# Queue order of the loads from the up projection into the first chunk of the down projection, and another order of one half unit's products

## Chip, cores and metric

One Trainium2 chip, one of its cores. The time is device microseconds of one execution of the whole layer; the kernel before takes 1906.95 us (median of 3 runs, 1906.23 to 1907.41).

## What is computed

One encoder layer on 512 tokens of width 2048, all in float32: attention and pooling with their projections, and a feed-forward part. The change lies in the feed-forward part:

```python
h = rms_norm(x, pre_ffn_g[l])
up = causal_dwconv(h @ w_up[l], conv_w[l], conv_b[l])
y = (jax.nn.gelu(up[..., :D_FF], approximate=True) * up[..., D_FF:]) @ w_down[l]
x = x + rms_norm(y, post_ffn_g[l])
```

Here `w_up` is 2048 x 11264 (`D_FF` is 5632) and `w_down` is 5632 x 2048.

## The kernel before

**Split products.** Every float32 product is made of three passes of TensorE: each factor is split into a rounded high part (ScalarE, L143) and the low rest (VectorE, L144), and `mm3` adds high x high (L159), low x high (L160) and high x low (L161). In the up projection from half unit 4 on, L947 and L953 do the same with wider matmuls for products 3 to 7.

**Up projection.** The output columns are cut into 88 half units (number k, from 0), each 128 channels, two half units to a unit. Each half unit is a 2 x 2 block product done with seven products instead of eight (Strassen's scheme in Winograd's form), numbered i = 1 to 7; below, (k, i) is product i of half unit k. The factor on the side of the weights is a block of `w_up`, or a sum of blocks. A buffer `wx` gets the block (1,1) by a plain DMA of the SP queue (L786), then further blocks by accumulating DMAs of the POOL queue (L795), each of which can start only when the split that reads the sum so far is done. So `wx` serves (k,4) or (k,5), then (k,6), then (k,3). Likewise `wy` holds (k,1), `wz` (k,2), `wv` the factor of (k,7) for k below 5, `ww` a plain copy for (k,4) in the first half units, and `wu` a plain copy that VectorE adds to `wx` or `wv` (L803) for (k,3) of half units 1, 2 and 3; in half units 2 and 3 it also adds `ww` to `wv` (L801). For half units 0 and 4 the last block of `wx` came by an accumulating DMA instead; from half unit 5 on VectorE adds `wz`.

**Order of the work.** `Factors.order` lists the products by hand; TensorE follows it, and each product's factor is split four products ahead (`AHEAD`), its loads asked for some six further ahead (`LOOK`). Half unit 4 is number `EARLY - 1`, the fifth: there the products go over from halves of single PSUM banks to pairs of banks, which VectorE must first have emptied (L1182 is the last reading of one of them). TensorE's order is written in the program; those of VectorE, ScalarE and the queues come from a scheduler that places the instructions by its own estimate, unless `tc.issue_after(x)` holds an instruction behind another. Each engine and each queue works in its order: an instruction that waits holds up all behind it. A load waits for its buffer: `raw4` has 6 of them, `wx` from half unit 2 on has 3.

**Down projection.** `w_down` is worked off in chunks, of which the first is chunk 0, with the same seven products in two column halves cc. `right` loads a factor of the weights (`b`, 1 MB each, from `in_w_down` or from sums made ahead in DRAM, `wd_sum`; L645 and L652), `left` and `first_left` load the gate products (`gc` and `a`, from `gd`; L1296 and L1197). The buffers of `b` come from a ring of 3 (`raw1`) and one of 2 (`raw2`). `ORDER0` gives the order for chunk 0: (0,1), (0,2), (1,1), (1,2), then 5, 7, 6, 3, 4 of each half. The first two products begin while the last products of half unit 87 are being finished on VectorE.

Of the kernel before, what the change touches and what calls it, by code (L numbers as in the profile page):

```python
# [30 lines left out]
EARLY = 5  # L31
# [46 lines left out]
def encoder_layer(ctx: ExitStack, tc: tile.TileContext, x, xT, vecs, rel, post_mix, post_ffn,  # L78
# [7 lines left out]
    nc = tc.nc  # L86
# [114 lines left out]
    def qk_specs(h):  # L201
        return halves(f"q{h}", w_in, head_cols("q", h), 8, P), halves(f"k{h}", w_in, head_cols("k", h), 8, P)
# [8 lines left out]
    for h in range(1, HEADS):  # L211
        q, k = qk_specs(h)
# [51 lines left out]
    for kb in range(KD):  # L264
        i, o = divmod(kb, 8)
# [329 lines left out]
    gd = [[dram.tile([P, CU, 2, H], F32, name=f"gd{c}_{i}") for i in range(2)] for c in range(NC)]  # L595
# [12 lines left out]
    def right_tile(tag, name, dt=F32R):  # L608

        n = turns[tag] = turns.get(tag, -1) + 1  # L610
        if later and n % (2 + LATER[tag]) >= 2:
            return later[tag](name, dt)
        return pr.tile([P, CU, S], dt, tag=tag, bufs=2, name=name)
# [3 lines left out]
    def raw1(name, dt=F32):  # L617
        return right_tile("raw1", name, dt)

    def w_block(j, l, c=0, cs=slice(0, C)):  # L620
        r = 256 * CU * c
        return w_down[r:r + 256 * CU, l * C + cs.start:l * C + cs.stop].rearrange(
            "(u j p) n -> p u j n", j=2, p=P)[:, :, j, :]

    wd_sum = {i: dram.tile([P, CU, C], F32, name=f"wd_sum{i}") for i in (5, 7, 6, 4)}
# [14 lines left out]
    def right(c, cc):  # L640
        cs = slice(cc * S, (cc + 1) * S)

        def load(j, l, ring=None):
            b = (ring or (later["raw2"] if j else raw1))(f"b{j}{l}")
            nc.sync.dma_start(b, w_block(j, l, c, cs))  # L645
            return b

        def first_chunk(i):
            if i in (1, 2):
                return ahead.pop((cc, i), None) or load(i - 1, 0, later[f"raw{i}"] if cc else raw1)  # L650
            b = (raw1 if i in (7, 3) else later["raw2"])(f"b{i}")
            nc.sync.dma_start(b, w_block(1, 1, c, cs) if i == 3 else wd_sum[i][:, :, cs])  # L652
            return b

        b = {}
        order = yield
        while True:
            i = order
            if i < 0:
                ahead[cc, -i] = first_chunk(-i)  # L660
                order = yield
                continue
            if c == 0:
                v = first_chunk(i)
            else:
                for jl in {1: (11, 12), 5: (11, 12), 7: (22,), 6: (22,), 3: (22,), 2: (21,), 4: (21,)}[i]:
                    if jl not in b:
                        b[jl] = load(jl // 10 - 1, jl % 10 - 1)
                for n, into, other in ((5, 11, 12), (7, 12, 22), (6, 11, 22), (4, 21, 11)):
                    if i == n:  # L670
                        nc.vector.tensor_add(b[into], b[into], b[other])  # L671
                v = b[{1: 11, 5: 11, 7: 12, 6: 11, 2: 21, 3: 22, 4: 21}[i]]
            hi, lo = right_tile("wh", "bh"), right_tile("wl", "bl")
            split(hi, lo, v)
            order = yield hi, lo
# [50 lines left out]
    class Factors:  # L726
# [3 lines left out]
        def __init__(self):  # L730
            n = 2 * NU

            self.order = [(k, i) for k in range(EARLY) for i in (1, 2)]
            self.order += [(0, 5), (0, 7), (1, 5), (0, 6), (1, 7), (1, 6), (0, 3), (1, 3), (0, 4), (1, 4)]
            self.order += [(j, i) for i in (4, 7, 5, 6, 3) for j in (2, 3)]
            for k in range(EARLY - 1, n):
                late = [(k - 1, 6), (k - 1, 3)]
                if k < EARLY:
                    o = [(k, 4), (k, 7), (k, 5)]
                elif k == n - 1:  # L740
                    o = [(k, 4), (k, 1), (k, 5), (k, 2), *late, (k, 6), (k, 7)]
                else:
                    o = [(k, 4), (k, 1), (k, 2), *late, (k, 5), (k, 7)]
                self.order += o
            self.order += [(n - 1, 3)]
            self.last = n - 1
            self.alone = *range(EARLY), n - 1
            self.raw, self.made, self.loaded, self.used = {}, [], 0, 0
            self.held = {"x": [], "r": []}
            self.homes = []  # L750
# [21 lines left out]
            self.add(k, "x", 1, 0)  # L772

        def load(self, k, i):
            what = "u" if i == 3 and k in (1, 2, 3) else self.source(k, i)
            if (k, what) in self.raw:
                return True
            in_x = what == "x" and k >= 2 or what == "w" and k == self.last
            held, n = (self.held["x"], 3) if in_x else (self.held["r"], 6)
            if len(held) >= n and held[-n] in self.raw:  # L780
                return False
            if in_x and p3 is None:
                return False
            held.append((k, what))
            v = raw_x("wx") if in_x else raw4("w" + what)
            self.last_load = nc.sync.dma_start(v, self.block(k, *self.LOADS[what])).ins  # L786
            self.raw[k, what] = v
            if what == "x" and k in self.alone:
                self.add(k, "x", 1, 0)
            if what == "v":  # L790
                self.add(k, "v", 0, 0)
            return True
# [4 lines left out]
        def make(self, k, i):  # L797
            early, what = k < EARLY, self.source(k, i)
            v = self.raw[k, what]
            if i == 6 and k in (2, 3):  # L800
                nc.vector.tensor_add(v, v, self.raw.pop((k, "w")))  # L801
            if i == 3 and k not in (0, 4):
                nc.vector.tensor_add(v, v, self.raw.pop((k, "u" if early else "z")))  # L803
            hi, lo = self.homes.pop(0) if self.homes else (w4("wfh"), w4("wfl"))
            split(hi, lo, v)
            if i == 4 and k not in self.alone:
                self.add(k, "x", 1, 0)
            elif i == 1 and not early:
                self.add(k, "y", 1, 0)
            elif i == 5 and k not in (2, 3):  # L810
                self.add(k, "x", 0, 0)
            elif i == 6 and k in (0, 4):
                self.add(k, "x", 0, 1)
            elif not (i == 6 or i == 2 and not early or i in (4, 7) and k in (2, 3)):
                del self.raw[k, what]
            self.made.append(tuple(v.rearrange("p (a b) -> p a b", a=8) for v in (hi, lo)))
# [32 lines left out]
    def raw_x(name):  # L849
        return p3.tile([P, 1024], F32, tag="x", bufs=3, name=name)  # L850
# [115 lines left out]
    with tc.tile_pool(name="p2", bufs=1, reuse_waits="tile") as p2:  # L966
# [112 lines left out]
        for n in (5, 3):  # L1079
            B = new_banks(f"m{n}", 4 if n == 5 else 0)  # L1080
            for cc in range(2):
                late = (lambda q: h0.append(next(turning))) if n == 3 else None
# [110 lines left out]
    def first_left():  # L1193

        def load(i, j):
            v = raw4(f"a{i}{j}").rearrange("p (u n) -> p u n", u=CU)
            nc.sync.dma_start(v, gd[0][i][:, :, j, :])  # L1197
            return v

        def parts(v):  # L1200
            hi, lo = (w4(f"a{p}").rearrange("p (u n) -> p u n", u=CU) for p in "hl")
            split(hi, lo, v)
            return hi, lo

        for j in range(2):
            yield parts(load(0, j))
# [68 lines left out]
    with tc.tile_pool(name="p4", bufs=2, reuse_waits="tile") as p4:  # L1275
# [16 lines left out]
        def left(c):  # L1292

            def load(i):
                g = half_g(f"gc{i}")
                nc.sync.dma_start(g, gd[c][i])  # L1296
                return [g[:, :, j, :] for j in range(2)]

            i = yield
            a11, a12 = load(0)  # L1300
            v, state = {1: a11, 2: a12, 3: a12}, None
            while True:
                if 7 not in v and (c or i not in (1, 2)):
                    a21, a22 = load(1)
                    s = scratch("s")
                    v.update({5: s, 7: a21, 6: s, 4: a22})
                if i in (5, 7) and state is None:
                    nc.vector.tensor_sub(s, a22, a21)
                    state = "n1"
                if i == 5 and state == "s2" or i == 6:  # L1310

                    nc.vector.scalar_tensor_tensor(s, s, -1.0, a11, op0=ALU.mult, op1=ALU.subtract)
                    state = "n1" if i == 5 else "s2"
                if i == 7:
                    nc.vector.tensor_sub(a21, a11, a21)
                if i == 3:
                    nc.vector.scalar_tensor_tensor(a12, a12, -1.0, s, op0=ALU.mult, op1=ALU.subtract)
                hi, lo = slot_h("ah", F32R), slot_l("al", F32R)
                split(hi, lo, v[i])
                i = yield hi, lo  # L1320
# [201 lines left out]
```

## Time and profile before

| what | value |
|---|---|
| median of 3 runs | 1906.95 us |
| profiled execution, its own time | 1911.16 us |
| its span, first to last instruction | 1909.2 us |
| mean granted TensorE clock | 0.993 |
| busy: VectorE | 1467.1 us, 77% |
| busy: ScalarE | 952.6 us, 50% |
| busy: POOL | 302.4 us, 16% |
| moved by DMA | 403.55 MB, mean 211 GB/s |

Times in the rows of the profile are microseconds from the span's start. A row of a timeline gives start, length, engine, line, operation, output and inputs, shapes, how many, and in brackets the idle time of the engine before it with what ended that. SPq and POOLq are the two DMA queues; "landing" is the time from issuing a DMA to its completion.

### The profile page before, as it was taken

Reading aid. Unit: us, or ns where it says so; the run is one execution under the profiler, and the core shown is the slowest. Engines: PE = TensorE matmul, PEld = TensorE weight load, DVE = VectorE, ACT = ScalarE, POOL = GpSimd, SP = SyncE. Lnnn points to the kernel's source line nnn. Section 1 sums busy time; section 2 is a strip of 40 time slices with the busy share of each in tenths; the row PEclk is TensorE's granted clock in tenths of the full one; section 3 lists DMA queues with packets and bytes.
Section 4 is the critical chain, followed back from the end, with each engine's and each line's share of the span. In section 5 each row is a group of like instructions: output and inputs, shape, how many; then the busy total and the mean of one; then the engine's idle time right before and its main releaser. Section 6 shows DMA issues by size and latency. Waiting matters only on the chain.

```text
span 1909.2 us, 26467 instructions
## 1 busy us (share of the span) xinstructions
PE 1873.5 (98%) x10298; PEld 1633.0 (86%) x10298; DVE 1467.1 (77%) x1742; ACT 952.6 (50%) x1174; POOL 302.4 (16%) x397
## 2 busy tenths in 40 slices
PE   9999999999999899999999999999998899999998
PEld 7888888888889889999999999999997688888886
DVE  5554346587688778888888888888888789998877
ACT  6333233355487445455455554455444555465543
POOL 4000000000001111111221112121110112222221
PEclk9999999999999989999999999999999999999999
DMA  9747948577877878788898889789776989999998
GB/s 329 216 116 177 246 110 207 142 192 222 279 278 193 233 162 202 201 195 189 196 202 223 195 184 222 191 185 203 178 167 208 326 242 250 251 221 240 222 225 236
DMA packets 181949, 403.55 MB, mean 211 GB/s; under 512 B 11584, under 2 KB 63168, under 8 KB 179264
## 3 DMA queue, kind: packets, MB, share of 16 engines
q0 software_dynamic: 47488, 144.72, 41.2%
q1 hardware_dynamic: 134336, 257.14, 40.9%
q8 instruction: 81, 1.33, 0.3%
q14 instruction: 44, 0.36, 0.1%
HBM read 345.19 MB, written 106.95 MB: 237 GB/s over the span
## 4 chain that ended last, share of the span: by engine, by line
PE 87%; DVE 5%; DMA 3%; issue 2%; ACT 2%; POOL 0%; SPq 0%; POOLq 0%; DVEq 0%; ACTq 0%
PE q L947 18%; PE q L953 9%; PE p L161 6%; PE p L159 6%; PE p L160 6%; PE q L160 6%; PE q L159 6%; PE q L161 6%; PE m L160 2%; PE m L159 2%; PE m L161 2%; PE u L160 2%; PE v L160 2%; PE u L161 2%; PE v L159 2%
## 5 line engine op out<-in xcount | busy, mean ns | idle before, releaser
L143 ACT ACTIVATE wfh<-wx 128x1024 fp32r<-128x1024 f32 x167 | 172.9, 1058 | 216.4 <-DVE wx L803 133.7
L947 PE MATMUL q<-h,wfh 128*128 128x512 f32 x960 | 255.7, 395 | 4.0 <-DVE z L1182 4.0
L144 DVE TENSOR_TENSOR wfl<-wx,wfh 128x1024 fp32r<-128x1024 f32 x167 | 200.7, 1221 | 57.9 <-ACT wfh L143 57.9
L159 PE MATMUL p<-bh,ah 128*128 128x512 f32 x560 | 219.2, 392 | 9.0 <-ACT ah L143 7.6
L161 PE MATMUL p<-bh,al 128*128 128x512 f32 x560 | 219.2, 391 | 3.3 <-DVE al L144 3.3
L160 PE MATMUL p<-bl,ah 128*128 128x512 f32 x560 | 218.8, 391 | 0.0
L159 PE MATMUL q<-gT,wfh 128*128 128x256 f32 x752 | 213.2, 283 | 1.1 <-DVE z L910 1.1
L161 PE MATMUL q<-gT,wfl 128*128 128x256 f32 x752 | 213.1, 283 | 0.9 <-DVE wfl L144 0.9
L160 PE MATMUL q<-gT,wfh 128*128 128x256 f32 x752 | 213.1, 283 | 0.0
L947 PEld LDWEIGHTS q<-h,wfh 128*128 128x128 f32 x960 | 176.6, 190 | 34.0 <-issue 4.3
L143 ACT ACTIVATE bh<-b 128x2048 fp32r<-128x2048 f32 x70 | 133.7, 1917 | 82.8 <-DVE b L671 51.3
L947 PE MATMUL q<-gT,wfh 128*128 128x512 f32 x640 | 169.4, 396 | 4.3 <-ACT wfh L143 3.2
L144 DVE TENSOR_TENSOR bl<-b,bh 128x2048 fp32r<-128x2048 f32 x70 | 159.5, 2287 | 13.8 <-PE p L160 7.4
L795 POOL DMA_DIRECT2D wx<-in_w_up x88 | 77.3, 878 | 547.2 <-DVE wfl L144 449.6
L160 PEld LDWEIGHTS q<-gT,wfh 128*128 128x128 f32 x752 | 142.3, 189 | 1.9 <-DVE gT L144 0.2
L159 PEld LDWEIGHTS q<-gT,wfh 128*128 128x128 f32 x752 | 142.4, 189 | 1.3 <-ACT wfh L143 1.3
L161 PEld LDWEIGHTS q<-gT,wfl 128*128 128x128 f32 x752 | 142.3, 189 | 1.3 <-DVE wfl L144 1.3
L947 PEld LDWEIGHTS q<-gT,wfh 128*128 128x128 f32 x640 | 119.7, 192 | 25.7 <-ACT wfh L143 3.5
L953 PEld LDWEIGHTS q<-h,wfl 128*128 128x128 f32 x960 | 131.8, 192 | 9.5
L143 ACT ACTIVATE wfh<-wy 128x1024 fp32r<-128x1024 f32 x82 | 87.1, 1062 | 102.6 <-PE q L953 66.0
L953 PE MATMUL q<-h,wfl 128*128 128x256 f32 x960 | 134.7, 283 | 0.0
L159 PEld LDWEIGHTS p<-bh,ah 128*128 128x128 f32 x560 | 105.6, 189 | 32.1 <-ACT ah L143 8.9
(441 smaller groups left out, 4132.2 us busy)
## 6 DMA issues: line engine op xcount, KB each, us to landing
wx<-in_w_up POOLq DMA_DIRECT2D x88, 512.0 KB, 7.4
b<-in_w_down SPq DMA_DIRECT2D x38, 1024.0 KB, 8.5
sum<-part POOLq DMA_DIRECT2D x70, 512.0 KB, 8.1
wx<-in_w_up SPq DMA_DIRECT2D x45, 512.0 KB, 4.2
wy<-in_w_up SPq DMA_DIRECT2D x44, 512.0 KB, 7.6
wz<-in_w_up SPq DMA_DIRECT2D x44, 512.0 KB, 3.8
wy<-in_w_up POOLq DMA_DIRECT2D x39, 512.0 KB, 7.7
wo_sum<-in_w_o POOLq DMA_DIRECT2D x16, 1024.0 KB, 12.0
```

The source lines that it names most:

```text
L143: rounded = nc.scalar.activation(hi, src, AF.Copy)
L144: nc.vector.tensor_sub(lo, src, f32(hi))
L159: nc.tensor.matmul(ps, l[0], r[0], start=first, stop=False)
L160: nc.tensor.matmul(ps, l[0], r[1], start=False, stop=False)
L161: nc.tensor.matmul(ps, l[1], r[0], start=False, stop=last)
L795: self.last_add = nc.gpsimd.dma_start(self.raw[k, what], self.block(k, m, kh), accum_op=ALU.add).ins
L947: nc.tensor.matmul(ps.rearrange("p (a b) -> p a b", a=2), w[0][:, kb], both(h_f[i], kb), start=kb == 0, stop=kb == 7)
L953: nc.tensor.matmul(ps[:, :T], w[1][:, kb], at(h_f[i], kb)[0], start=False, stop=False)
```

## The change

`in_turn` issues a DMA of the SP queue behind the one that it issued last, so that these DMAs stand in the queue in the order in which the program asks for them. All loads of `Factors.load`, of `first_left`, and those of `right` and `left` for chunk 0 go through it. In `Factors.order`, (4,5) and (5,4) move ahead of (4,7). For (4,3), `wu` is loaded by the SP queue, and VectorE adds it to `wx`; the accumulating DMA after (4,6) is gone. Nothing else changes; lines of the program from L625 on move down by 8.

```diff
+    def in_turn(dest, src):
+
+        with tc.issue_after(in_turn.last):
+            in_turn.last = nc.sync.dma_start(dest, src).ins
+        return in_turn.last
+
+    in_turn.last = load_w.last
+
...
         def load(j, l, ring=None):
             b = (ring or (later["raw2"] if j else raw1))(f"b{j}{l}")
-            nc.sync.dma_start(b, w_block(j, l, c, cs))
+            (nc.sync.dma_start if c else in_turn)(b, w_block(j, l, c, cs))
             return b
...
             b = (raw1 if i in (7, 3) else later["raw2"])(f"b{i}")
-            nc.sync.dma_start(b, w_block(1, 1, c, cs) if i == 3 else wd_sum[i][:, :, cs])
+            in_turn(b, w_block(1, 1, c, cs) if i == 3 else wd_sum[i][:, :, cs])
             return b
...
                 if k < EARLY:
-                    o = [(k, 4), (k, 7), (k, 5)]
+                    o = [(k, 4), (k, 5), (k + 1, 4), (k, 7)]
...
                 else:
-                    o = [(k, 4), (k, 1), (k, 2), *late, (k, 5), (k, 7)]
+                    o = [(k, 4), (k, 1), (k, 2), *late, (k, 5), (k, 7)][k == EARLY:]
...
-            what = "u" if i == 3 and k in (1, 2, 3) else self.source(k, i)
+            what = "u" if i == 3 and k in (1, 2, 3, 4) else self.source(k, i)
...
-            self.last_load = nc.sync.dma_start(v, self.block(k, *self.LOADS[what])).ins
+            self.last_load = in_turn(v, self.block(k, *self.LOADS[what]))
...
-            if i == 3 and k not in (0, 4):
+            if i == 3 and k:
                 nc.vector.tensor_add(v, v, self.raw.pop((k, "u" if early else "z")))
...
-            elif i == 6 and k in (0, 4):
+            elif i == 6 and not k:
                 self.add(k, "x", 0, 1)
...
-            nc.sync.dma_start(v, gd[0][i][:, :, j, :])
+            in_turn(v, gd[0][i][:, :, j, :])
...
-                nc.sync.dma_start(g, gd[c][i])
+                (nc.sync.dma_start if c else in_turn)(g, gd[c][i])
```

How the instructions move, at three places. First the SP queue of the kernel before, from the `wv` of (2,7) and (3,7) on: `wx` of half units 2 and 3 stands between the two `wu`, then `wx` of 4, 5 and 6 in one go, then `ww` and `wv` of half unit 4.

```order
L786 DMA wv<-in_w_up 128x1024 x2
L786 DMA wu<-in_w_up 128x1024
L786 DMA wx<-in_w_up 128x1024 x2
L786 DMA wu<-in_w_up 128x1024
L786 DMA wx<-in_w_up 128x1024 x3
L786 DMA ww<-in_w_up 128x1024
L786 DMA wv<-in_w_up 128x1024
L786 DMA wy<-in_w_up 128x1024
L786 DMA wz<-in_w_up 128x1024
```

The same stretch of the SP queue with the change: `wx` of 2 and 3, both `wu`, `ww` of 4, `wx` of 4 and 5, `wv` of 4, `wy` and `wz` of 5, then the new `wu` of 4.

```order
L623 DMA wv<-in_w_up 128x1024 x2
L623 DMA wx<-in_w_up 128x1024 x2
L623 DMA wu<-in_w_up 128x1024 x2
L623 DMA ww<-in_w_up 128x1024
L623 DMA wx<-in_w_up 128x1024 x2
L623 DMA wv<-in_w_up 128x1024
L623 DMA wy<-in_w_up 128x1024
L623 DMA wz<-in_w_up 128x1024
L623 DMA wu<-in_w_up 128x1024
L623 DMA wx<-in_w_up 128x1024
```

So `wx` of 2 and 3 moved ahead of a `wu`, and `wx` of 4 behind `ww` of 4; `wx` of 6 no longer stands ahead of `ww` and `wv`.

Second, VectorE where TensorE passes to pairs of banks, before: rows from the addition of (2,6)'s result on; `wfl<-wv` is the low part of (4,7), the two `wfl<-wx` are those of (4,5) and (5,4).

```order
L925 TENSOR_TENSOR z<-q_2_5585,z 128x512
L144 TENSOR_TENSOR wfl<-wv,wfh 128x1024
L928 TENSOR_TENSOR z<-q_2_5585,z 128x256
L925 TENSOR_TENSOR z<-q_3_5623,z 128x512
L1182 TENSOR_TENSOR z<-q_2_5524,z 128x512
L928 TENSOR_TENSOR z<-q_3_5623,z 128x256
L144 TENSOR_TENSOR wfl<-wx,wfh 128x1024
L1148 SCALAR_TENSOR_TENSOR ca<-z,vec,ca 128x511 x2
L1149 SCALAR_TENSOR_TENSOR ca<-z,vec,ca 128x510 x2
L144 TENSOR_TENSOR wfl<-wx,wfh 128x1024
```

The same rows of VectorE with the change.

```order
L933 TENSOR_TENSOR z<-q_2_5590,z 128x512
L144 TENSOR_TENSOR wfl<-wx,wfh 128x1024
L936 TENSOR_TENSOR z<-q_2_5590,z 128x256
L933 TENSOR_TENSOR z<-q_3_5623,z 128x512
L1190 TENSOR_TENSOR z<-q_2_5524,z 128x512
L936 TENSOR_TENSOR z<-q_3_5623,z 128x256
L144 TENSOR_TENSOR wfl<-wx,wfh 128x1024
L1156 SCALAR_TENSOR_TENSOR ca<-z,vec,ca 128x511 x2
L1157 SCALAR_TENSOR_TENSOR ca<-z,vec,ca 128x510 x2
L144 TENSOR_TENSOR wfl<-wv,wfh 128x1024
```

The splits of (4,5) and (5,4) took the places of those of (4,7) and (4,5), and (4,7) the third. Nine rows further on VectorE has one new row, the addition of `wu` to `wx` (L811 there, L803 before).

Third, the SP queue where the down projection begins, before, with the buffers' numbers: `b00` and `b10` of the top two rows of `b` are (0,1) and (0,2), `b3_13708` is (0,3), `b7_13825` is (1,7), `b00_13584` is (1,1), `b10_13603` is (1,2), `b5` is (0,5).

```order
L1197 DMA a00_13412<-gd0_0_3583 128x4x256
L1197 DMA a01_13472<-gd0_0_3583 128x4x256
L786 DMA wx_13072<-in_w_up 128x1024
L645 DMA b00_13280<-in_w_down 128x4x512
L645 DMA b10_13282<-in_w_down 128x4x512
L652 DMA b3_13708<-in_w_down 128x4x512
L652 DMA b7_13825<-wd_sum7_3611 128x4x512
L645 DMA b00_13584<-in_w_down 128x4x512
L1296 DMA gc0_13590<-gd0_0_3583 128x2048
L645 DMA b10_13603<-in_w_down 128x4x512
L652 DMA b5_13613<-wd_sum5_3610 128x4x512
L1296 DMA gc1_13619<-gd0_1_3584 128x2048
```

The same stretch of the SP queue with the change.

```order
L623 DMA wx_13074<-in_w_up 128x1024
L623 DMA wz_13077<-in_w_up 128x1024
L623 DMA b00_13282<-in_w_down 128x4x512
L623 DMA b10_13284<-in_w_down 128x4x512
L623 DMA a00_13414<-gd0_0_3583 128x4x256
L623 DMA a01_13474<-gd0_0_3583 128x4x256
L623 DMA b00_13586<-in_w_down 128x4x512
L623 DMA gc0_13592<-gd0_0_3583 128x2048
L623 DMA b10_13605<-in_w_down 128x4x512
L623 DMA b5_13615<-wd_sum5_3610 128x4x512
L623 DMA gc1_13621<-gd0_1_3584 128x2048
L623 DMA b7_13629<-wd_sum7_3611 128x4x512
```

The loads for (0,3) and (1,7) no longer stand ahead of those for (1,1), `gc0`, (1,2), (0,5) and `gc1`, and the two `a` moved from ahead of (0,1) and (0,2) to behind them. Between the two places, each `wx` of a half unit k now stands ahead of its own `wy` and `wz`, where before it stood ahead of those of k + 1.

## Prediction

> **What bounds it now.** I read the page first, then the windows, then TensorE's timeline where its windows are not full, and last the engines and queues that it waits for there.
>
> ```profile
> PE 1873.5 (98%) x10298; PEld 1633.0 (86%) x10298; DVE 1467.1 (77%) x1742; ACT 952.6 (50%) x1174; POOL 302.4 (16%) x397
> ```
>
> TensorE is the bound; only its idle time and its slow clock can be won. The windows (span, then busy time of PE, PEld, DVE, ACT, POOL with counts, granted clock, DMA share, GB/s) say where these lie:
>
> ```profile
> 655.00:705.00 50.00, 42.46 (x241) 37.85 (x240) 32.01 (x44) 20.99 (x25) 7.60 (x9) 0.86 0.73 166
> 1460.00:1515.00 55.00, 44.02 (x174) 33.38 (x175) 40.79 (x35) 30.07 (x29) 5.41 (x8) 0.94 0.92 322
> 850.00:950.00 100.00, 100.00 (x651) 91.50 (x651) 84.36 (x107) 50.97 (x59) 21.14 (x25) 1.00 0.87 196
> 1445.00:1460.00 15.00, 13.67 (x80) 11.81 (x79) 13.62 (x19) 9.53 (x10) 0.00 (x0) 1.00 0.10 24
> ```
>
> In 655 to 705 TensorE is idle for 7.5 us and its clock is 0.86; in 1460 to 1515 it is idle for 11.0 us. Between the two (850 to 950 stands for it) it is full. In 1445 to 1460 the DMA engines do almost nothing (share 0.10), right ahead of the second hole. TensorE's timeline in the first hole:
>
> ```profile
> 659.92 1.78 PE L947 MATMUL q<-h,wfh 128*128 128x512 f32 x7
> ...
> 666.86 3.33 PE L947 MATMUL q<-h,wfh 128*128 128x512 f32 x7 [3.98 <-DVE z L1182]
> ...
> 678.61 0.39 PE L161 MATMUL q<-gT,wfl 128*128 128x256 f32 x1 [0.39 <-DVE wfl L144]
> ...
> 684.22 1.78 PE L947 MATMUL q<-h,wfh 128*128 128x512 f32 x7
> ...
> 690.34 3.36 PE L947 MATMUL q<-gT,wfh 128*128 128x512 f32 x7 [3.16 <-ACT wfh L143]
> ...
> 701.30 2.00 PE L947 MATMUL q<-h,wfh 128*128 128x512 f32 x8
> ```
>
> (4,4) begins at 659.92. Then TensorE waits 3.98 us, and (4,7) runs at half clock (3.33 us for seven matmuls that took 1.78 before). (5,1) gets its low part at 678.61. (4,6) begins at 684.22; behind it 3.16 us are lost, and (4,3) is slow again. The last row is the end of (5,7) and the start of (6,4). Who was late, on VectorE, ScalarE, the SP queue and the POOL queue:
>
> ```profile
> 639.96 1.29 DVE L1165 TENSOR_TENSOR ca<-ca,cb 128x512 f32<-128x512 f32 x2 [2.46 <-ACT ca L1158]
> ...
> 643.77 2.35 DVE L801 TENSOR_TENSOR wv<-wv,ww 128x1024 f32<-128x1024 f32 x2
> ...
> 663.95 1.23 DVE L144 TENSOR_TENSOR wfl<-wv,wfh 128x1024 fp32r<-128x1024 f32 x1 [8.24 <-ACT wfh L143]
> ...
> 677.34 1.22 DVE L144 TENSOR_TENSOR wfl<-wy,wfh 128x1024 fp32r<-128x1024 f32 x1
> ...
> 679.61 1.22 DVE L144 TENSOR_TENSOR wfl<-wx,wfh 128x1024 fp32r<-128x1024 f32 x1
> ```
>
> ```profile
> 636.50 1.06 ACT L143 ACTIVATE wfh<-wx 128x1024 fp32r<-128x1024 f32 x1 [2.81 <-DMA wx<-in_w_up]
> ...
> 662.87 1.06 ACT L143 ACTIVATE wfh<-wv 128x1024 fp32r<-128x1024 f32 x1 [9.93 <-DMA wv<-in_w_up]
> ...
> 689.23 2.00 ACT L143 ACTIVATE wfh<-wx 128x1024 fp32r<-128x1024 f32 x2 [11.80 <-DMA wx<-in_w_up]
> ```
>
> ```profile
> 604.32 12.82 SPq L786 DMA_DIRECT2D wv<-in_w_up  x2
> 621.59 0.90 SPq L786 DMA_DIRECT2D wx<-in_w_up  x2
> ...
> 645.02 0.33 SPq L786 DMA_DIRECT2D ww<-in_w_up  x1
> ```
>
> ```profile
> 653.07 0.92 POOL L795 DMA_DIRECT2D wv<-in_w_up  x1 [9.71 <-DMA wv<-in_w_up]
> ```
>
> L1182, which (4,7) waits for, stands on VectorE behind the low part of (4,7) itself (663.95, after 8.24 us of nothing), that behind ScalarE's high part (662.87), and that waited for the accumulate on `wv` issued at 653.07: 9.8 us. (4,3) waited 11.80 us on ScalarE for the last accumulate on `wx`.
>
> **The change, part by part.** Landings (min, median, max) of the loads of `w_up` in 640 to 665 and of its accumulates in 640 to 700:
>
> ```profile
> DMA to landing us min/median/max: 4.5/5.9/8.6
> DMA to landing us min/median/max: 5.6/6.6/9.7
> ```
>
> *First gap.* L1182 now stands behind the split of (4,5), whose `wx` needs a load and one accumulate. The load comes right behind `ww`, and `ww` waits for the first of the two L801 (643.77; `ww` went out at 645.02). That L801 gets earlier: VectorE waited 2.46 us at 639.96 for ScalarE's gelu (L1158), which stood behind a high part that waited 2.81 us for `wx` of half unit 2 (636.50). That `wx` was issued at 621.59, behind a `wu`; now it follows the second `wv`, issued at 604.32 + 12.82 - 0.33 = 616.8, so it comes over 4 us earlier and the wait goes. `ww` then goes out at 642.5, `wx` of 4 at 642.9 (0.4 for one issue), lands 5.9 later; 0.4 more for the POOL queue, then the accumulate, 8.5 (near the one of 9.8, which ran beside the same loads): 657.7. VectorE starts the low part 1.1 later (as 662.87 to 663.95), at 658.8 instead of 663.95. From there to the end of the low part of (5,1) it takes what it took, 677.34 + 1.22 - 663.95 = 14.6: 673.4. TensorE could be there at 659.92 + 4 products of 2.79 (below) = 671.1, so it waits 2.3 us at (5,1), and the term is 673.4 - 678.6 = **-5.2**. Bounds: -7.5 where TensorE doesn't wait; with the gelu still late and both DMAs at their longest (645.4 + 8.6 + 0.4 + 9.7 + 1.1 = 665.2), +1.2. (5,4), now second, has a plain load, which lands before. (4,7), now third, is asked for 5.6 us later than it was, and its accumulate has that time more.
>
> *Second gap.* No accumulate is left after (4,6): VectorE adds `wu`, which has landed long before, in 1.2 us, then high part 1.0, low part 1.2. Behind the low part of (4,6) (679.61 + 1.22) that is 684.3 on the times before, and (4,3) is needed at the end of (4,6), 687.0. The addition costs nothing: ScalarE, and VectorE behind it, did nothing while waiting for 689.23. From 684.22, four products of 2.79 would end at 695.4; (6,4) began at 701.5 (its row starts with the last matmul of (5,7)). Term: **-6.1**, of which 3.16 is idle and 3.0 slow clock. Bound: if the wait of 2.3 us at (5,1) halves the clock again, -3.1. Of the idle times 3.16 halved it and 1.05 (1491.32, below) did not; 2.3 lies between, and I take none.
>
> The half units up to 87 follow with nothing moved on VectorE, ScalarE or POOL, so TensorE hands on what it has won. In the second hole, TensorE, the SP queue and VectorE:
>
> ```profile
> 1444.38 1.77 PE L947 MATMUL q<-h,wfh 128*128 128x512 f32 x7
> ...
> 1447.17 1.77 PE L947 MATMUL q<-gT,wfh 128*128 128x512 f32 x7
> ...
> 1470.62 0.39 PE L161 MATMUL p<-bh,al 128*128 128x512 f32 x1
> 1476.10 0.79 PE L159 MATMUL p<-bh,ah 128*128 128x512 f32 x1 [5.09 <-ACT ah L143]
> ...
> 1477.95 0.79 PE L161 MATMUL p<-bh,al 128*128 128x512 f32 x1 [0.34 <-DVE al L144]
> ...
> 1481.11 0.52 PE L159 MATMUL p<-bh,ah 128*128 128x512 f32 x1
> ...
> 1491.32 0.50 PE L159 MATMUL p<-bh,ah 128*128 128x512 f32 x1 [1.05 <-ACT ah L143]
> ...
> 1514.05 0.50 PE L161 MATMUL p<-bh,al 128*128 128x512 f32 x1 [0.53 <-DVE al L144]
> ```
>
> ```profile
> 1433.93 1.09 SPq L645 DMA_DIRECT2D b<-in_w_down  x2
> 1457.93 0.37 SPq L652 DMA_DIRECT2D b<-in_w_down  x1
> 1463.32 0.54 SPq L652 DMA_DIRECT2D b<-wd_sum  x1
> 1463.95 0.56 SPq L645 DMA_DIRECT2D b<-in_w_down  x1
> ```
>
> ```profile
> 1469.62 1.28 DVE L1165 TENSOR_TENSOR ca<-ca,cb 128x512 f32<-128x512 f32 x2
> 1474.47 2.29 DVE L144 TENSOR_TENSOR bl<-b,bh 128x2048 fp32r<-128x2048 f32 x1 [3.57 <-ACT bh L143]
> ```
>
> One product takes 1447.17 - 1444.38 = 2.79. The third product of the down projection, (1,1), should follow 1470.62; it waits 5.09 us for `gc0`, and the clock is low until 1481.11. The SP queue shows why: the loads for (0,3) and (1,7) waited there until 1457.93 and 1463.32 for the buffers of (0,1) and (0,2), with the loads for (1,1), `gc0`, (1,2), (0,5) and `gc1` behind them. By the waits in the built program these five need only buffers that (87,5) and (87,2) leave, and TensorE is past both at 1444.38. So they go out some 18 us earlier, into the idle stretch.
>
> *Third gap.* Then VectorE decides: it finishes L1165 at 1470.90, the low part of `b` takes 2.29 (1474.47), that of `gc0` 1.2: 1474.4, where the third matmul of (1,1) began at 1477.95. That is -3.6; without low clock afterwards 0.9 more (ten matmuls took 1481.11 - 1477.95 = 3.16 us, at 0.23 they take 2.3). The wait, 3.1 us in two pieces, is nearest to the 3.16 that halved the clock, so I take **-3.6**; bounds 0 (loads no earlier) and -4.5.
>
> *Later gaps.* Six more (first and last quoted) leave 11.0 - 5.09 - 0.34 = 5.6 us. They wait for splits behind late loads and for VectorE. The five loads are now ahead of need, but VectorE's additions (L701) still wait for the DMAs that write the products: I take 2 us as left, **-3.6**, bounds 0 and -5.6.
>
> At nothing: the two `a` now go out behind two `b` (1433.93), but were used by ScalarE only after 1449; `wx` ahead of `wy` and `wz` in the half units between is the rival of the other side.
>
> On the clock, the Trainium skill (TensorE: Matmul & The Clock Gate, Part 1) says that it halves after an idle window of about 3.4 us, free-running. By that rule neither new wait would halve it, and the sum would be lower by 0.9; the row of 3.16 us speaks against so sharp a limit.
>
> Sum: -5.2 - 6.1 - 3.6 - 3.6 = -18.5. The profiled execution, 1911.2 (span 1909.2 and 2.0 around it), becomes 1892.7; it lies 4.2 above the median of the runs, so the median of 1906.95 becomes **1888.5**.
>
> **Rivals.** A measurement of this kernel can tell about 0.2%, 3.8 us, from no change.
>
> 1. *VectorE takes over in the down projection.* It was busy 41 of 55 us there, so it has room, but its order is fixed and it waits inside it. Third and later gaps then give 2 instead of 7.2: 1893.7. Chance 0.13.
> 2. *The accumulate for (4,5) is no earlier.* `ww`, `wx` of 4 and 5 and `wv` now go out within 1.2 us, and the accumulate of `wx` shares the engines with them and with that of `wv`. First term +1.2, and a clock that stays slow (-3.1): 1897.9. For it speaks the accumulate of 9.8 us, against it that this one ran beside the same loads. The Trainium skill (DMA: Bandwidth & Descriptors, Issuing engines are not separate DMA queues) has it that DMAs of all queues share the same 16 engines and interleave. Chance 0.13.
> 3. *Order of issue is not order of landing*, and the queue's order changes little: only VectorE's addition acts, -6 at most, or the waits move on and nothing is seen: 1901 to 1907. Against it: what held the loads up in the SP queue was the issuing, by 14 us and more. Chance 0.06.
> 4. *Slower: the `wx` of each half unit holds up `wy` and `wz`.* They now stand in the queue until (k-3,3) is split and a `wx` buffer is free. From there to the split of (k,1) are 11 products, 30.7 us; a landing takes up to 9.7. So it costs nothing unless that distance falls under 10 us; from then on 1 us for each of 39 half units, less the 18.5, makes 1927.5. Chance 0.04.
>
> **The numbers.** The forecast has 0.64. The range, 1883 to 1899, goes from all terms at their best (-7.5 - 6.1 - 4.5 - 5.6 = -23.7, 1883.3) to just past rival 2. It leaves out 3, 4 and mixtures of 1 with 2. Faster by over 0.2%: 0.64 + 0.13 + 0.13 and a third of rival 3, 0.92; within 0.2%: 0.04; slower: 0.04.
>
> **What would show it.** Right: no idle time of TensorE over 1 us between 655 and 671, one of about 2 us at (5,1), none ahead of (4,3), (6,4) some 11 us earlier; the SP queue issuing the loads of (1,1) to `gc1` before TensorE ends half unit 87; the third product waiting for VectorE's L144, not for ScalarE. Wrong: ScalarE waiting for a DMA of `wx` ahead of (4,5) until 662 or later; TensorE waiting in the half units between; the five loads going out in time and TensorE idle as before.

## The result, and the profile after

| | median of the runs | lowest to highest | runs |
|---|---|---|---|
| before | 1907.18 us | 1906.23 to 1909.38 | 4 |
| changed | 1897.05 us | 1893.71 to 1898.80 | 4 |

The ratio is 0.9943, with a 95% interval of 0.9926 to 0.9960: some 10 us faster. The forecast was 1888.5 us, 18.5 us faster; the time lies inside the range that was given, but little more than half of the expected gain came. The profiled execution of the changed kernel took 1897.62 us.

The engines on the page, then the windows of the first hole, of the stretch ahead of the second, and of the second (columns as before: span, busy time of PE, PEld, DVE, ACT, POOL, clock, DMA share, GB/s):

```profile
PE 1870.9 (99%) x10298; PEld 1631.7 (86%) x10298; DVE 1467.0 (77%) x1743; ACT 952.6 (50%) x1174; POOL 301.4 (16%) x396
```

```profile
655.00:705.00 50.00, 47.58 (x305) 43.42 (x304) 40.35 (x52) 25.95 (x30) 7.62 (x9) 0.97 0.76 202
950.00:1400.00 450.00, 450.00 (x2923) 411.70 (x2922) 382.45 (x480) 227.16 (x261) 87.83 (x104) 1.00 0.79 196
1440.00:1455.00 15.00, 13.68 (x72) 11.54 (x71) 13.88 (x17) 7.68 (x8) 0.00 (x0) 1.00 0.73 292
1455.00:1515.00 60.00, 54.26 (x216) 43.34 (x215) 44.02 (x37) 34.69 (x32) 8.03 (x10) 0.91 0.78 263
```

The first hole has shrunk from 7.5 us idle to 2.4, and its clock is 0.97 instead of 0.86. Between the holes TensorE is full, as before. The idle stretch of the DMA engines is gone (share 0.73, it was 0.10). But the second hole still has 5.7 us idle, and its clock is lower than before (0.91). TensorE's timeline names each of the gaps:

```profile
658.94 1.78 PE L955 MATMUL q<-h,wfh 128*128 128x512 f32 x7
...
667.11 2.22 PE L955 MATMUL q<-h,wfh 128*128 128x512 f32 x7 [2.42 <-DVE z L884]
...
680.12 1.78 PE L955 MATMUL q<-h,wfh 128*128 128x512 f32 x7
...
691.07 2.00 PE L955 MATMUL q<-h,wfh 128*128 128x512 f32 x8
...
1448.89 0.50 PE L159 MATMUL p<-bh,ah 128*128 128x512 f32 x1 [1.32 <-DVE t L890]
...
1462.22 0.50 PE L160 MATMUL p<-bl,ah 128*128 128x512 f32 x1 [1.93 <-DVE bl L144]
1463.36 0.50 PE L161 MATMUL p<-bh,al 128*128 128x512 f32 x1 [0.63 <-DVE al L144]
...
1483.95 0.56 PE L160 MATMUL p<-bl,ah 128*128 128x512 f32 x1 [2.60 <-DVE bl L144]
1485.09 0.79 PE L161 MATMUL p<-bh,al 128*128 128x512 f32 x1 [0.57 <-DVE al L144]
...
1543.92 0.50 PE L160 MATMUL p<-bl,ah 128*128 128x512 f32 x1 [1.55 <-DVE bl L144]
```

The 1.32 us ahead of the down projection's first matmul were there before (1.33). Four other waits are left: one at (5,4) (667.11), one at the third product of the down projection, (1,1), one at the sixth, (0,7), and a new one far behind the second hole, at the second product of chunk 1 (1543.92). To see what each is worth, the same points of TensorE's work in both kernels, from the first profiled execution of each and from a second one of each (the last two experiments); the products of the down projection are counted off at 24 matmuls each:

| point | before | changed | moved | second pair |
|---|---|---|---|---|
| (4,6) begins | 684.22 | 680.12 | -4.1 | 683.18 to 679.74, -3.4 |
| row with the start of (6,4) | 701.30 | 691.07 | -10.2 | 698.11 to 690.69, -7.4 |
| first matmul of the down projection | 1459.84 | 1448.89 | -11.0 | 1456.43 to 1448.32, -8.1 |
| third matmul of its third product | 1477.95 | 1463.36 | -14.6 | 1474.44 to 1462.78, -11.7 |
| its ninth product | 1519.21 | 1503.90 | -15.3 | 1517.56 to 1501.11, -16.5 |
| its 27th product (in chunk 1) | 1617.13 | 1604.35 | -12.8 | 1615.48 to 1605.22, -10.3 |
| span | 1909.2 | 1895.8 | -13.4 | 1907.1 to 1896.7, -10.4 |

The up projection and the third product gain. What is gained after that, up to the ninth product, is given back by the 27th, and more.

### The profile page after: what moved, and what is told of

It is laid out like the page before. It is cut to its first block, busy times and chain, and to the rows that moved or that the text cites. A ratio compares the mean times of both kernels' runs of the same rounds, so it can differ in the third digit from the quotient of the medians.

```text
span 1895.8 us, 26426 instructions
## 1 busy us (share of the span) xinstructions
PE 1870.9 (99%) x10298; PEld 1631.7 (86%) x10298; DVE 1467.0 (77%) x1743; ACT 952.6 (50%) x1174; POOL 301.4 (16%) x396
## 3 DMA queue, kind: packets, MB, share of 16 engines
q8 instruction: 81, 1.33, 0.3%
## 5 line engine op out<-in xcount | busy, mean ns | idle before, releaser
L144 DVE TENSOR_TENSOR wfl<-wx,wfh 128x1024 fp32r<-128x1024 f32 x167 | 200.8, 1222 | 51.8 <-ACT wfh L143 51.7
L144 DVE TENSOR_TENSOR bl<-b,bh 128x2048 fp32r<-128x2048 f32 x70 | 159.3, 2285 | 9.5 <-PE p L160 5.2
L803 POOL DMA_DIRECT2D wx<-in_w_up x87 | 76.5, 879 | 532.0 <-DVE wfl L144 446.2
L160 PEld LDWEIGHTS p<-bl,ah 128*128 128x128 f32 x560 | 106.2, 190 | 30.3 <-DVE bl L144 8.3
```

Source lines behind the costliest of these rows:

```text
L144: nc.vector.tensor_sub(lo, src, f32(hi))
L160: nc.tensor.matmul(ps, l[0], r[1], start=False, stop=False)
L803: self.last_add = nc.gpsimd.dma_start(self.raw[k, what], self.block(k, m, kh), accum_op=ALU.add).ins
```

## Experiments

The kernel before took 1907.62 us (21 runs), 1907.42 (15) and 1907.96 (9) beside the three groups of experiments. Ratios are to it, as recorded with their 95% intervals; they can differ a little from the quotient of the two medians.

**The order of the products and VectorE's addition for (4,3), with no load queued in turn.** Below, the two together are called the order; they were not tried apart.

```diff
-            self.last_load = in_turn(v, self.block(k, *self.LOADS[what]))
+            self.last_load = nc.sync.dma_start(v, self.block(k, *self.LOADS[what])).ins
...
-                (nc.sync.dma_start if c else in_turn)(g, gd[c][i])
+                nc.sync.dma_start(g, gd[c][i])
```

(and the same in `right` and `first_left`)

> The fifth half unit's other order and VectorE's addition for (4,3), with every load queued as in the kernel before. In the trace of before, the wx of half unit 4 was issued at 624.19 and its accumulate had landed at 642.78; with the change it was issued at 642.65 and the accumulate landed at 656.92. Theory A: the order of the products alone closes the first hole, and queueing the up projection's loads in turn delays that wx. Then the low part of (4,5) starts before 656, TensorE does not wait at (5,4), its clock stays at 1.00 up to 705, and (6,4) starts near 688 (changed kernel: 691.07, before: 701.30); the holes of the down projection stay as before; about 13 us under the kernel before. Rival B, the step of the prediction: the loads have to come in turn for (4,5) to be early; then (4,5) is late again, (6,4) starts at 694 or later and at most 7 us are gained.

Measured: 1897.13 us (1895.98 to 1899.04), ratio 0.9944 (0.9931 to 0.9956): as fast as the whole change. Its window of the first hole, and its SP queue and VectorE there:

```profile
655.00:705.00 50.00, 50.00 (x332) 45.99 (x331) 43.92 (x58) 26.43 (x31) 8.46 (x10) 1.00 0.87 222
```

```profile
624.34 19.99 SPq L794 DMA_DIRECT2D wx<-in_w_up  x3
```

```profile
655.75 1.22 DVE L144 TENSOR_TENSOR wfl<-wx,wfh 128x1024 fp32r<-128x1024 f32 x1
```

TensorE has no gap and full clock, and the row with (6,4) begins at 687.93, where 688 was expected and the whole change has 691.07. The row of the SP queue begins at 624.34 with `wx` of half unit 4, as in the kernel before; the changed kernel issues it at 642.65. So the first hole is closed without any load in turn, and Rival B falls: queueing the up projection's loads in turn isn't needed for it, it takes some of it back.

**The up projection's part alone.** The change, with the loads of `right`, `first_left` and `left` issued as before.

> The whole change in the up projection, the down projection's loads queued as before. Theory A: (6,4) starts at 691.07 as with the change, the later part is that of the kernel before (third product waiting some 5 us), no gap in chunk 1; about 11 us less in the trace, 8 to 11 in the median, and slower than the order alone by 2 to 3 us. Rival B: the same 11 us, and faster than the order alone by 4 us or more.

Measured: 1905.06 us (1902.47 to 1909.04, 11 runs), ratio 0.9989 (0.9980 to 0.9998). Both theories had (6,4) early, and it is (691.61). Both missed what follows; TensorE in the first hole and at the end of the up projection, then ScalarE and the SP queue of this kernel:

```profile
667.67 3.21 PE L955 MATMUL q<-h,wfh 128*128 128x512 f32 x7 [3.05 <-DVE z L884]
...
1432.04 3.03 PE L955 MATMUL q<-gT,wfh 128*128 128x512 f32 x7 [4.23 <-DVE t L890]
```

```profile
1424.09 1.06 ACT L143 ACTIVATE wfh<-wx 128x1024 fp32r<-128x1024 f32 x1 [6.67 <-DMA wx<-in_w_up]
```

```profile
1410.60 1.28 SPq L1205 DMA_DIRECT2D a<-gd  x2
```

A wait of 4.23 us and a slow clock stand at 1432, where no other kernel waits more than 1.13 us: ScalarE waited 6.67 us for the accumulate on a `wx`. The two `a`, which stand behind two `b` where the down projection's loads are queued in turn too, were issued at 1410.60, right ahead of this accumulate and the one before it, which then took 10.3 and 8.9 us to land (7.0 and 7.3 for such a pair in the kernel before). That the `a` slowed them is argued from these times, not tried by itself. Queueing the up projection's loads in turn without those of the down projection is 8 us slower than queueing both; the other way round it is not so (the fourth experiment).

**The down projection's part alone.** The kernel before, with `in_turn` in `right`, `first_left` and `left` for chunk 0.

> Only the loads of the down projection's first chunk in turn, the up projection as before. Theory A: the third product's third matmul comes 3.6 us earlier, of which the wait at (0,7), behind VectorE's addition that waits for the DMA writing (1,1), and VectorE's new order in chunk 1 take back about 2; 1 to 3 us less in all. Rival C, the prediction's sum: 7.2 us less. Rival D: what is lost in chunk 1 belongs to the times, not to the order, and does not show here; 4 to 5 us less.

Measured: 1905.48 us (1903.49 to 1905.90, 11 runs), ratio 0.9983 (0.9974 to 0.9992): 2.1 us less in the medians and some 3 by the ratio (1.5 to 5.0), Theory A's size and not the 7.2 of the prediction's sum. The times alone don't rule out the 4 to 5 of Rival D; the trace does, for the new gap in chunk 1 is there. The third product comes early:

```profile
1470.81 0.49 PE L160 MATMUL p<-bl,ah 128*128 128x512 f32 x1 [1.93 <-DVE bl L144]
...
1551.38 0.80 PE L160 MATMUL p<-bl,ah 128*128 128x512 f32 x1 [2.43 <-DVE bl L144]
```

**The change without the queueing in the up projection.**

```diff
-            self.last_load = in_turn(v, self.block(k, *self.LOADS[what]))
+            self.last_load = nc.sync.dma_start(v, self.block(k, *self.LOADS[what])).ins
```

> The change without the queueing of the up projection's loads: other order, VectorE's addition, and the down projection's loads in turn. Theory A: the sum of the first and the third run, about 15 us under the kernel before and 2 to 3 us under the changed kernel (1897.05), so near 1894. Rival B: 5 us or more above the changed kernel.

Measured: 1893.98 us (1891.78 to 1895.31), ratio 0.9924 (0.9912 to 0.9937), as Theory A put it. In medians: order -10.5, down projection in turn a further -3.1, up projection in turn +3.1, which leaves the change at the order's own gain. Each step of 3 us is smaller than the intervals are wide (some 5 us), so their sizes are not settled. For the last one the traces agree: this kernel has (6,4) at 687.75, the changed kernel at 691.07.

**The bank for (5,4) cleared first.** The gelu waits for L883, the split of (4,7) for L884.

```diff
+        if u == PAIRED // 2 - 1:
+            begin_z(PAIRED)
+            with tc.issue_after(begin_z.act):
+                nc.scalar.activation(flat(a), flat(a), AF.Gelu_apprx_tanh)
+            return a
...
+            if (k, i) == (PAIRED, 7):
+                with tc.issue_after(begin_z.dve):
+                    split(hi, lo, v)
```

> The changed kernel, with the clearing of (4,2)'s bank (L883 on ScalarE, L884 on VectorE) ahead of the gelu and of the split of (4,7). Theory A: the 2.42 us that TensorE waits at (5,4) are made by what stands ahead of L883 and L884 on ScalarE (gelu, 1.06) and VectorE (low part of (4,7), 1.2); the wait falls to about 1.3, the clock is no longer halved behind it, (6,4) starts at about 688.4 instead of 691.07; 2 to 3 us under the changed kernel. Rival E: (5,4) waits for its own factor; nothing moves. Rival F: the wait falls and the clock is halved all the same; 1 us.

The rows behind this, of the changed kernel on VectorE and ScalarE:

```profile
658.12 1.22 DVE L144 TENSOR_TENSOR wfl<-wx,wfh 128x1024 fp32r<-128x1024 f32 x1 [3.39 <-ACT wfh L143]
...
664.90 1.22 DVE L144 TENSOR_TENSOR wfl<-wv,wfh 128x1024 fp32r<-128x1024 f32 x1
...
666.64 0.42 DVE L884 TENSOR_TENSOR z<-q,z 128x256 f32<-128x256 f32 x1
```

```profile
665.08 1.06 ACT L1166 ACTIVATE ca<-ca 128x1024 f32<-128x1024 f32 x1 [1.69 <-DVE ca L1157]
666.04 0.37 ACT L883 ACTIVATE z<-q 128x256 f32<-128x256 f32 x1
```

(5,4) writes to a pair of banks of which one bank still holds (4,1) and (4,2). L883 and L884 take it away, into a buffer that comes free after L1157, and they stand behind the gelu (L1166) and the split of (4,7). With them ahead, TensorE in this experiment:

```profile
665.02 1.89 PE L959 MATMUL q<-h,wfh 128*128 128x512 f32 x7 [0.82 <-DVE z L888]
...
687.92 2.00 PE L959 MATMUL q<-h,wfh 128*128 128x512 f32 x8
...
1480.44 0.79 PE L160 MATMUL p<-bl,ah 128*128 128x512 f32 x1 [2.79 <-DVE bl L144]
...
1541.34 0.56 PE L160 MATMUL p<-bl,ah 128*128 128x512 f32 x1 [2.73 <-DVE bl L144]
```

The wait falls to 0.82, the clock stays up, (6,4) begins at 687.92: the place is as Theory A had it. The time is not: 1897.26 us (1895.96 to 1898.41), ratio 0.9946 (0.9933 to 0.9958), no better than the change. The first matmul of the down projection is 3.7 us earlier than with the change (1445.22), the last matmul 1.7; 2.0 us of the gain are lost between the third product and chunk 1, where the waits are 2.79 and 2.73. Why the medians show no gain at all stays open.

**A fresh buffer for the addition of (1,2).**

```diff
-            if i == 2 and order_of(c, cc) is LAST_ORDER:
+            if i == 2 and ((c, cc) == (0, 1) or order_of(c, cc) is LAST_ORDER):
                 v = later["part"]("part")
```

> The changed kernel, with product (1,2) added into a fresh buffer instead of the one from which (1,1) is still being written to memory. Theory A: VectorE's addition waits for that DMA (landed at 1480.91, addition at 1481.01), and the split for (0,7) stands behind it; the wait of 2.60 + 0.57 us at (0,7) and the half clock behind it go, the seventh product of the down projection starts 3 to 5 us earlier against the third; how much of it is left at the end depends on the gap in chunk 1, 1 to 4 us in all. Rival G: the addition waits for TensorE, which the trace names; the wait stays.

The rows of the changed kernel behind it, POOL's write of (1,1) (landed at 1480.91) and VectorE's addition:

```profile
1471.18 0.71 POOL L720 DMA_DIRECT2D sum<-part  x1 [2.31 <-ACT part L713]
```

```profile
1481.01 0.69 DVE L709 TENSOR_TENSOR part<-p,part 128x512 f32<-128x512 f32 x1 [7.43 <-PE p L160]
1481.61 2.28 DVE L144 TENSOR_TENSOR bl<-b,bh 128x2048 fp32r<-128x2048 f32 x1
```

The trace names TensorE, but the product that L709 reads was done by 1475.53, where the next begins. With a fresh buffer, VectorE in the experiment waits 1.41 us, for that product, and the split of (0,7) follows 8 us earlier, 6 of them against the third product:

```profile
1472.97 0.69 DVE L709 TENSOR_TENSOR part<-p,part 128x512 f32<-128x512 f32 x1 [1.41 <-PE p L161]
1473.58 2.28 DVE L144 TENSOR_TENSOR bl<-b,bh 128x2048 fp32r<-128x2048 f32 x1
```

TensorE has no gap at (0,7), and its seventh product starts 6.7 us earlier against the third, more than the 3 to 5 expected. Measured: 1894.10 us (1890.90 to 1896.42), ratio 0.9931 (0.9918 to 0.9945), 3 us under the change in the medians, with intervals that overlap. Theory A holds, Rival G falls: the wait was for the DMA.

**All chunks in turn.** On the kernel of the fourth experiment (the change without the queueing in the up projection; called the fourth kernel), `in_turn` for every chunk in `right` and `left`.

> The fourth run's kernel (up projection's loads as before, other order, first chunk in turn) with the loads of all chunks in turn, which puts L1320 on VectorE behind the two additions of b for the second product of chunk 1. Theory A: the 3.10 us at that product are VectorE's order; with 1.2 us less ahead of it the gap falls to about 1.9 or below; 1 to 4 us under the fourth run's kernel (1893.98). Rival H: the gap is made by the load of b (issued at 1526.12 behind a split, landed at 1533.32), or comes back further on; no change.

Measured: 1903.24 us (1901.18 to 1906.26, 11 runs), ratio 0.9976 (0.9968 to 0.9985), 9 us slower than the fourth kernel. The gap in chunk 1 fell to 1.21 us, as Theory A had it, but others opened:

```profile
1539.56 0.50 PE L160 MATMUL p<-bl,ah 128*128 128x512 f32 x1 [1.21 <-DVE bl L144]
...
1628.60 0.50 PE L160 MATMUL p<-bl,ah 128*128 128x512 f32 x1 [1.71 <-DVE bl L144]
```

The last matmul of the down projection comes 3.2 us later than in the fourth kernel, and from there to the end of the span it takes 56.4 us instead of 51.9. Rival H had the gain come back further on, and it does; but no expectation had the kernel slower, and what makes the last stage longer was not looked into.

**In turn for half units 0 to 3 alone**, on the fourth kernel.

```diff
-            self.last_load = nc.sync.dma_start(v, self.block(k, *self.LOADS[what])).ins
+            self.last_load = (in_turn if k < 4 else dma_ins)(v, self.block(k, *self.LOADS[what]))
```

> The fourth run's kernel with the up projection's loads in turn for half units 0 to 3 alone, so that wx of 2 and 3 come ahead of a wu, and wx of 4 stays early. Theory A: ScalarE no longer waits 2.8 us for wx of 2, and the gap of 0.94 us near 642 goes; about 1 us under the fourth run's kernel, at the edge of what can be measured. Rival B: queueing in turn costs as it did for half unit 4; 2 us or more above it.

Measured: 1890.78 us (1890.45 to 1894.81), ratio 0.9917 (0.9904 to 0.9931). The gap near 642 is gone, and (4,4) begins at 657.57 instead of 659.74. The interval overlaps with the fourth kernel's, so the size (some 1 to 3 us) is not settled; the place is.

**Both together**: the eighth kernel with the fresh buffer.

> The eighth run's kernel with the fresh buffer of the sixth for product (1,2). Theory A: the waits at (0,7), 1.18 and 0.63 us there, go, and with them the slow clock behind them; 2 to 3 us under the eighth run's kernel (1890.78), so 1888 to 1889, unless the gap in chunk 1 grows by as much. Rival I: the gap in chunk 1 is set by loads that don't come earlier, and takes all of it back; 1890 to 1891.

Measured: 1888.67 us (1887.90 to 1889.52), ratio 0.9900 (0.9886 to 0.9913), 8 us under the changed kernel and 2 under the eighth, as Theory A put it: the best of these kernels. Both holes of its windows:

```profile
655.00:705.00 50.00, 50.00 (x325) 45.67 (x325) 43.15 (x56) 27.99 (x33) 9.31 (x11) 1.00 0.85 209
1460.00:1515.00 55.00, 55.00 (x244) 45.55 (x243) 38.91 (x29) 30.93 (x28) 8.73 (x10) 1.00 1.01 350
```

The gap in chunk 1 (3.09 us) is still there.

**VectorE's order at the start of chunk 1.** The ninth kernel, with L679 of the third product and L1320 held behind the low part of the second product's `b`.

> The ninth run's kernel with VectorE's order at the start of chunk 1 held: low part of the second product's b ahead of the next addition of b, and L1320 behind it. Theory A: the gap of some 3 us at the second product of chunk 1 is VectorE's order; it falls to under 1 us there, 2 to 4 us less if nothing behind it is late in its turn. Rival J: the scheduler's further order changes with it and new gaps open behind; no gain, or slower.

Measured: 1896.59 us (1893.84 to 1896.90), ratio 0.9935 (0.9921 to 0.9948), 8 us slower than the ninth kernel. TensorE:

```profile
1531.53 0.50 PE L160 MATMUL p<-bl,ah 128*128 128x512 f32 x1 [0.93 <-DVE bl L144]
1539.33 0.50 PE L160 MATMUL p<-bl,ah 128*128 128x512 f32 x1 [2.05 <-DVE bl L144]
...
1576.46 0.50 PE L159 MATMUL p<-bh,ah 128*128 128x512 f32 x1 [2.83 <-ACT bh L143]
```

The gap moves on to later products (Rival J). This order on VectorE doesn't help; that VectorE is late there whatever its order is likely by it, not shown.

**Both kernels profiled again.**

> The kernel before, profiled a second time. Theory A: its profiled execution of 1911.16 us was an unlucky one of a spread of some 5 us, and this one lies nearer to the median of 1907, with the same places of waiting.

> The changed kernel, profiled a second time: (6,4), the third product of the down projection, the waits at (0,7) and in chunk 1 at the same places within 1 us of their size; the difference between the two second profiles is nearer to the 10 us of the medians than to the 13.5 of the first ones.

1908.96 us and 1898.58 us. The second profile of the kernel before has smaller holes in the up projection:

```profile
665.80 3.32 PE L947 MATMUL q<-h,wfh 128*128 128x512 f32 x7 [3.55 <-DVE z L1182]
...
688.30 2.91 PE L947 MATMUL q<-gT,wfh 128*128 128x512 f32 x7 [2.17 <-ACT wfh L143]
```

In the first profile these waits were 3.98 and 3.16 us, and the down projection began 3.4 us later. In the second profile of the changed kernel the places are the same, not all sizes within 1 us: 3.06 us at (5,4), 1.37 and 0.64 at (0,7), 3.08 in chunk 1 (with 2.42, 2.60 and 0.57, 1.55 in the first). The two second profiles differ by 10.4 us.

## Why the prediction was right and wrong, step by step

**First gap: right in its rows, wrong in the place of the wait.** The low part of (4,5) began at 658.12 (forecast 658.8), that of (5,1) was done at 672.7 (forecast 673.4). But TensorE waited at (5,4), not at (5,1): the step looked at the factors alone and missed that (5,4), moved ahead, needs a pair of banks that L884 still had to clear. And the step "I take none" for the clock failed: behind 2.42 us (5,4) took 2.22 us for seven matmuls instead of 1.78, and what follows was slower still. (4,6) came 4.1 us earlier (3.4 in the second pair), for 5.2.

**A term that was taken the wrong way round.** The prediction has `wx` of 4 go out at 642.9 and land early enough, and it did. It didn't see that the kernel before had this `wx` complete at 642.78, as its POOL queue shows, and that the queueing in turn is what made it late: with the change the accumulate landed at 656.92. The order without it (first experiment) has (6,4) 3.1 us earlier. The accumulate on this `wx`, before and with the change:

```profile
634.19 0.86 POOL L795 DMA_DIRECT2D wx<-in_w_up  x1 [1.36 <-DMA wx<-in_w_up]
```

```profile
647.69 0.92 POOL L803 DMA_DIRECT2D wx<-in_w_up  x1 [7.12 <-DMA wx<-in_w_up]
```

**Second gap: right, for the execution that was profiled.** From (4,6) to (6,4) it was 17.1 us and is 11.0: -6.1, as forecast. In the second profile of the kernel before it was 14.9, with a shorter wait there (2.17 us), so in the second pair the change wins 4.0.

**Third gap: right.** -3.64 (second pair -3.55) for -3.6, with the wait in two pieces, on VectorE's L144, and the half clock behind it, as the step had it: the ten matmuls from the third one on take 3.98 us before and 3.99 with the change. (The step counted ten matmuls up to 1481.11, where the trace of the kernel before has seven. At full clock these would save 1.6 us, not 0.9, so the step's lower bound should have been near -5.2; the forecast doesn't use it.) The five loads went out from 1430.76 to 1437.66, 29 to 33 us earlier than before, and 18 to 22 beyond what the start moved; the first and the last of them:

```profile
1430.76 3.10 SPq L623 DMA_DIRECT2D b<-in_w_down  x1
...
1437.66 1.12 SPq L623 DMA_DIRECT2D gc<-gd  x1
```

**Later gaps: wrong as a sum.** Forecast -3.6; between the third matmul of (1,1) and the 27th product 1.8 us were lost in the first pair and 1.4 in the second. Up to the ninth product, where the gaps of this step lay, it came to -0.7 and -4.8; from there to the 27th, in chunk 1, 2.5 and 6.2 us were lost, which no term had. Two waits make this. The step said that L701's additions still wait for the DMAs that write the products, and priced this at 2 us. The wait alone is 3.17 us in two pieces at (0,7) in the first profile (2.01 in the second), and the clock is slow behind it. The sixth experiment shows that this DMA makes it. The other wait is the gap in chunk 1, which the step didn't look for. ScalarE in the changed kernel waits there for chunk 1's first `gc`, and VectorE for ScalarE:

```profile
1523.24 1.06 ACT L143 ACTIVATE ah<-gc 128x1024 fp32r<-128x1024 f32 x1 [5.85 <-DMA gc<-gd]
```

```profile
1524.33 1.23 DVE L144 TENSOR_TENSOR al<-gc,ah 128x1024 fp32r<-128x1024 f32 x1 [7.22 <-ACT ah L143]
```

```profile
1501.23 0.52 SPq L623 DMA_DIRECT2D b<-wd_sum  x1
1506.34 0.37 SPq L653 DMA_DIRECT2D b<-in_w_down  x1
1506.77 1.33 SPq L1304 DMA_DIRECT2D gc<-gd  x2
```

That `gc` now stands behind the `b` of (1,4) and a second `b` of chunk 1 (the first two rows), ahead of which it stood before; it landed at 1523.21, 74.3 us after the down projection's first matmul (before: 1519.74, 59.9 us after). Of these 14.4 us, 3.7 are a later issue and 10.7 a slower landing (16.4 us from issue to landing instead of 5.7). VectorE, idle for 7.22 us ahead of it, then works almost without a pause until the gap at 1543.92 and after. All kernels with chunk 0 in turn have this gap (0.9 to 3.1 us), and in all of them VectorE waits 6.6 to 8.3 us ahead of it, at the low part of this `gc`; those without have neither. The load's place was not changed by itself, so this cause is argued, not shown; that the other order on VectorE in the tenth experiment doesn't cure it is shown. The prediction followed the SP queue only as far as the loads that it wanted early, not to those that they were moved past.

**From one execution to the median.** The sum was made against an execution 4.2 us above the median, and all of this was taken off as if it lay elsewhere. The second profile, 2.2 us shorter in all, begins the down projection 3.4 us earlier, and 3.2 of these are there by (6,4): what made the first execution long lay for the most part in the holes that the change closes anyway. So 13.4 us in the first pair of traces are 10.4 in the second and 10.1 in the medians.

**Together.** In the first pair: 1.1 us missing in the first gap, 5.4 in the later ones, 1.3 won at the end of the up projection and in the last stage that no term had: -18.5 becomes -13.4; the unlucky execution makes -10.1 of it.

**Rivals:** the first, VectorE in the down projection, came nearest: it had the third and later gaps at 2 us together, and they gave 1.8 and 2.2. Rival 2 fell (the accumulate landed at 656.92, the split began at 658.12), rival 3 as well (the loads did land early), and rival 4: TensorE is full from 950 to 1400. The range held partly by luck: its upper end was put just past rival 2, whose 1897.9 us is nearly the measured time, though the late accumulate that it rests on didn't occur.

## What to carry to other kernels

Where a change gives a queue another order, follow the order to its end and ask of each transfer that others were moved ahead of how much later it lands; one of them may be the one that an engine without slack needs. A product moved ahead needs its output banks earlier too, not only its factors. Before a hole of one profile is priced, profile the kernel twice: what an execution lies above the median may lie in that very hole.

## What was not expected of the hardware

In these traces, whether the clock halves behind a wait is not told by the wait's length alone. After 2.42 us at (5,4) it halved (the window's clock is 0.97), after 1.77 us at the same place in the sixth experiment it did not (1.00); after 2.64 us in chunk 1 in the eighth it did not, after 1.93 and 0.63 us in the changed kernel it did:

```profile
1464.47 0.63 PE L161 MATMUL p<-bh,al 128*128 128x512 f32 x1
1464.90 0.63 PE L159 MATMUL p<-bh,ah 128*128 128x512 f32 x1
...
1467.58 0.40 PE L160 MATMUL p<-bl,ah 128*128 128x512 f32 x1
1467.81 0.39 PE L161 MATMUL p<-bh,al 128*128 128x512 f32 x1
```

Starts 0.43 us apart are the half clock, 0.23 us the full one. The same two waits (1.92 and 0.64 us) in the ninth kernel left the clock at 1.00 in the window quoted above. So a wait of 2 to 3 us costs no more than itself in one execution and some 2.4 us more in another (behind 1485.09 twelve matmuls of the changed kernel start 0.43 apart, 0.2 more each). This fits the spread between runs of one kernel: the four of the changed kernel were the shorter the higher their mean granted clock, from 1893.71 us at 0.997 to 1898.80 at 0.994. The Trainium skill (TensorE: Matmul & The Clock Gate, Part 1) has an activity window of about 3.4 us that is free-running, so that what a kernel sees depends on its phase. The run-to-run part agrees with these rows; that an idle time has to reach 3.4 us does not, since 2.42 us, and 1.93 with 0.63 behind it, were enough.
